# A hybrid attention layer in fp32: FF weight sums issued two per split in the attention stages, and the first gate's activation sums made in the GLA stage

## The chip, the cores and the metric

The kernel runs on one core of one Trainium2 chip, in one launch. The metric is the device time of that launch in microseconds, as the median of the runs. TensorE is called PE here, VectorE DVE, ScalarE ACT, GpSimd POOL and SyncE SP, as in the profile.

## What is computed

One layer of a streaming encoder, batch 1, 512 frames, width 1024, all in float32. Three branches read the same normalised input and are merged by gates; an FF block follows.

```python
u = rmsnorm(h, g_mix)
(gq, gk, gv, gg, ga, fq, fk, fv, ff, mq, gates) = split_cols(u @ w_in, PROJ_SIZES)
o_gla = gla_chunk_causal(gq, gk, gv, log_a)          # 4 heads, dk 64, dv 128
y_gla = (rmsnorm(o_gla, g_gla_head) * silu(gg)) @ w_gla_o
y_fox = forgetting_attention(fq, fk, fv, log_f) @ w_fox_o      # 8 heads of 64
y_mem = memory_attention(mq, mk, mv) @ w_mem_o       # 4 heads, 256 memory tokens
gt = sigmoid(gates)                                  # 3 gates of width 1024
merged = gt[0] * y_gla + gt[1] * y_fox + gt[2] * y_mem
h = h + merged @ w_out
u2 = rmsnorm(h, g_ffn)
h = h + square(relu(u2 @ w_ff1)) @ w_ff2
out = rmsnorm(h, g_final)
```

## The kernel before

**Precision.** Every fp32 product is made of three matmuls in `float32r` (`mm3`, L165 to L167): an operand x is split into hi = cast(x) and lo = x - hi, and hi*hi, hi*lo and lo*hi are added up in PSUM. A weight chunk is 128 x 1024 numbers, 512 KB. `load_w` (L148) loads it on SP's queue into `raw`, ACT casts `hi` (L155), DVE subtracts `lo` (L156). The three tags each have a ring of three tiles. The split of one chunk is followed by `next_sum` (L117), of which more below. The splits are counted from 1 (`chunk_n`).

**Stages.** The order of the program: the memory keys and values and the norm of x ("front"); FoX (`xp`); memory attention (`ap`); the GLA stage (`lp`); the gate stage (`op_`); FF (`yp`). In FoX, memory attention and the GLA stage, generators of projections (`gT`, `gN`, `outputs`) are woven with the steps of the attention (`weave`), in an order written out by hand, and ACT, DVE and SP follow program order as far as the scheduler leaves it. In the gate stage, `in_order` (L133) chains DVE, ACT and SP in program order. POOL's order is the scheduler's.

**The gate stage.** The three gates (fox, mem, gla, g = 0 to 2) are products of 512 x 1024 by 1024 x 1024, each made as seven products of half the size (Strassen in Winograd's form). `rounds` holds the order: (g, n) with n in (1, 2, 5, 3, 6, 7, 4), for g = 0, 1, 2, then ("Y", 1), (2, 4), ("Y", 0), ("O", 1), ("O", 0), where Y is the `w_gla_o` product and O the `w_out` product. A round of a gate has two weight chunks c, each with 24 matmuls for its tokens. The weights of rounds 1, 2 and 3 are blocks of `w_in`, the others are sums of blocks, made in two pairs of tiles `wb`: `load_sum` (L1060, SP) loads "11" or "12" into a tile, `plus` (L1063) adds another block by an accumulating DMA on POOL, and each round's split (`high` L1078 on ACT, `low` L1082 on DVE) reads the tile. In the first gate, `first_sum` (L1183) makes the first sum on DVE (`vec`, L1039) out of the two loaded tiles. The activations have sums too: S1 to S4 are splits (`left`, L1035 and L1036) of sums of the quarters of u, of which `sum_four` and `sum_three` make two. What of this is loaded and made in which round stands in the tables `loads`, `early` and `after`, filled by `at` and run round by round; in each round the evictions (`evac`), the tanh and the merges of the round before come in between.

**FF weight sums.** FF is Winograd too, and its weight sums are made in DRAM ahead of it: `sum_ops` (L107) lists for each of five blocks q eight DMAs on POOL, four copies and four accumulates, into the tensors T1 to T4. Blocks q = 1, 2, 3 take 1024 KB a DMA, q = 0 and 4 take 512 KB; 40 DMAs in all. `next_sum` issues one of them at each split from the eighth on, with a wait on that split's cast ("pace", L118 to L130). The list is cut in three: the first 32, then 4 from round (2, 6) on, the last 4 from round Y0 on, where two go with each split.

The sums are read in FF, where T is loaded like a weight (L1385).

## Time and profile before

| | us |
|---|---|
| median of 3 runs | 834.33 (832.12 to 834.57) |
| the profiled execution | 834.19 |
| its span | 832.4 |
| outside the span | 1.8 |

| stretch of the span | us, about |
|---|---|
| front | 0 to 45 |
| FoX | 45 to 158 |
| memory attention | 158 to 232 |
| GLA stage | 232 to 293 |
| first gate | 293 to 350 |
| second and third gate, Y and O | 350 to 490 |
| FF | 490 to 832 |

The page has, from the top: the busy time of each engine; the span in 40 slices of 20.8 us with one digit for tenths of busy time, the granted TensorE clock, and the DMA share; the DMA queues (q0 holds what POOL issues, q1 what SP and others issue by hardware); the chain of work that ended last; the groups of instructions by line and tile names. A row such as "PE mm L165 <- ACT ct L1133: 3.0, 1, 3.0" reads: PE waited at line 165 for ACT's line 1133, 3.0 us in total, once, at most 3.0. In the chain each row is a start, a duration and what ran.

### The profile page before, as it was taken

What the parts mean: (1) busy time and instruction counts of PE and PEld (TensorE: products, weight loads), DVE (VectorE), ACT (ScalarE), POOL (GpSimd) and SP (SyncE); (2) the same over time, 40 slices, a digit from 0 to 9 for tenths busy, and PEclk for the clock granted to TensorE, in tenths of its full rate; (3) what the DMA queues carried; (4) which work ended last, traced back from release to release, by engine and by line L of the source; (5) the groups of instructions that cost most, each with busy time, mean ns of one, the idle gap of its engine ahead of it and who ended that gap; (6) DMA issues with size and microseconds to landing.
All of it is one profiled execution on the core that took longest, in us unless ns stands there. A gap on an engine that the chain in (4) does not pass through costs nothing.

```text
span 832.4 us, 11709 instructions
## 1 busy us (share of the span) xinstructions
PE 805.4 (97%) x4375; PEld 685.6 (82%) x4375; DVE 609.3 (73%) x945; ACT 460.6 (55%) x733; POOL 101.2 (12%) x135
## 2 busy tenths in 40 slices
PE   9999999999999996988999999999999999999996
PEld 7788888888888874766888889998998899889985
DVE  6868887376455764746756656889799779888896
ACT  7757565434543433633553435786577366747764
POOL 0001010101011202123411000011001100110011
PEclk9999999999999997999999999999999999999998
DMA  9355565689586899885978642698867975896644
GB/s 358 130 171 177 178 178 159 186 238 278 138 230 190 263 247 228 210 177 163 216 177 284 187 149 76 214 283 184 264 195 160 219 238 173 192 233 230 172 79 128
DMA packets 40778, 165.44 MB, mean 199 GB/s; under 512 B 4881, under 2 KB 5585, under 8 KB 38353
## 3 DMA queue, kind: packets, MB, share of 16 engines
q0 software_dynamic: 10784, 61.87, 35.4%
q1 hardware_dynamic: 28576, 98.86, 33.8%
q10 hardware_dynamic: 1360, 3.96, 1.4%
q8 instruction: 34, 0.56, 0.3%
q14 instruction: 24, 0.19, 0.1%
HBM read 162.55 MB, written 35.68 MB: 238 GB/s over the span
## 4 chain that ended last, share of the span: by engine, by line
PE 83%; DMA 7%; DVE 4%; issue 3%; ACT 1%; POOL 1%; SPq 0%; POOLq 0%; DVEq 0%; ACTq 0%
PE mm L1317 15%; PE mm L165 14%; PE mm L167 14%; PE mm L166 14%; PE a L166 5%; PE a L167 5%; PE a L165 5%; DMA wb<-in_wst_dram 4%; PE mm L1646 3%; DMA raw<-in_wst_dram 1%; PE mm L1647 1%; DMA xt<-in_xT_dram 1%; DVE lo L1082 1%; PE mm L606 1%; PE a L399 1%
## 5 line engine op out<-in xcount | busy, mean ns | idle before, releaser
L1376 ACT CAST hi<-raw 128x1024 fp32r<-128x1024 f32 x52 | 54.5, 1048 | 36.9 <-PE mm L1317 16.2
L1377 DVE TENSOR_TENSOR lo<-raw,hi 128x1024 fp32r<-128x1024 f32 x52 | 63.6, 1224 | 14.4 <-ACT hi L1376 14.2
L156 DVE TENSOR_TENSOR wlo<-raw,whi 128x1024 fp32r<-128x1024 f32 x38 | 46.5, 1224 | 33.1 <-ACT whi L155 32.9
L1317 PE MATMUL mm<-u,hi 128*128 128x256 f32 x384 | 65.1, 283 | 0.0
L155 ACT CAST whi<-raw 128x1024 fp32r<-128x1024 f32 x38 | 39.9, 1050 | 41.3 <-PE mm L166 14.5
L165 PE MATMUL mm<-uhl,whi 128*128 128x512 f32 x144 | 57.8, 402 | 0.0
L1696 POOL DMA_DIRECT2D b<-in_wst_dram x30 | 25.6, 854 | 261.2 <-DVE lo L1377 130.3
L1317 PEld LDWEIGHTS mm<-u,hi 128*128 128x128 f32 x384 | 56.8, 191 | 0.3
L167 PE MATMUL mm<-uhl,wlo 128*128 128x512 f32 x144 | 56.3, 391 | 0.0
L166 PE MATMUL mm<-uhl,whi 128*128 128x512 f32 x144 | 56.2, 390 | 0.0
L165 PE MATMUL mm<-hi,ch 128*128 128x512 f32 (+1 forms) x132 | 50.9, 386 | 0.0
L166 PE MATMUL mm<-lo,ch 128*128 128x512 f32 (+1 forms) x132 | 50.9, 386 | 0.0
L167 PE MATMUL mm<-hi,cl 128*128 128x512 f32 (+1 forms) x132 | 50.9, 386 | 0.0
L1082 DVE TENSOR_TENSOR lo<-wb,hi 128x1024 fp32r<-128x1024 f32 x21 | 29.4, 1414 | 25.3 <-ACT hi L1078 25.2
L1317 PE MATMUL mm<-u2s,hi 128*128 128x256 f32 x288 | 47.6, 283 | 0.0
L1317 PE MATMUL mm<-u,lo 128*128 128x256 f32 x192 | 47.5, 283 | 0.0
L1376 ACT CAST hi<-b 128x1024 fp32r<-128x1024 f32 x26 | 27.3, 1049 | 29.5 <-PE mm L167 19.4
L1078 ACT CAST hi<-wb 128x1024 fp32r<-128x1024 f32 x28 | 28.6, 1046 | 25.8 <-DMA wb<-in_wst_dram 20.3
L1317 PEld LDWEIGHTS mm<-u2s,hi 128*128 128x128 f32 x288 | 41.8, 192 | 0.3
L1377 DVE TENSOR_TENSOR lo<-b,hi 128x1024 fp32r<-128x1024 f32 x26 | 31.7, 1224 | 10.9 <-ACT hi L1376 10.8
L166 PE MATMUL a<-lo,ch 128*128 128x512 f32 (+1 forms) x96 | 37.0, 385 | 0.0
L165 PE MATMUL a<-hi,ch 128*128 128x512 f32 (+1 forms) x96 | 37.0, 385 | 0.0
(501 smaller groups left out, 2335.9 us busy)
## 6 DMA issues: line engine op xcount, KB each, us to landing
raw<-in_wst_dram SPq DMA_DIRECT2D x110, 512.0 KB
raw<-T SPq DMA_DIRECT2D x32, 512.0 KB
b<-in_wst_dram POOLq DMA_DIRECT2D x32, 512.0 KB, 5.6
T<-in_wst_dram POOLq DMA_DIRECT2D x12, 1024.0 KB, 9.5
wb<-in_wst_dram POOLq DMA_DIRECT2D x22, 512.0 KB, 7.2
b<-in_wst_dram SPq DMA_DIRECT2D x16, 512.0 KB
T<-in_wst_dram POOLq DMA_DIRECT2D x12, 512.0 KB, 5.2
wb<-in_wst_dram SPq DMA_DIRECT2D x12, 512.0 KB
```

Of the source, the lines that this page charges most:

```text
L155: cast = nc.scalar.copy(hi, raw)
L156: low_now[0] = nc.vector.tensor_tensor(lo, raw, f(hi), op=ALU.subtract).ins
L165: nc.tensor.matmul(ps, lh, rh, start=start, stop=False, skip_group_check=on)
L166: nc.tensor.matmul(ps, lh, rl, start=False, stop=False, skip_group_check=on)
L167: nc.tensor.matmul(ps, ll, rh, start=False, stop=stop, skip_group_check=on)
L1078: next_sum(nc.scalar.copy(ws[r, c][0], source(r, c)).ins)
L1082: nc.vector.tensor_tensor(lo, source(r, c), f(hi), op=ALU.subtract)
L1317: nc.tensor.matmul(ps[:, a, :], x[:, a, k, :], y[:, s, k, :], start=start, stop=stop, skip_group_check=go is not None)
L1376: split_now[0] = nc.scalar.copy(hi, raw).ins
L1377: split_now[1] = nc.vector.tensor_tensor(lo, raw, f(hi), op=ALU.subtract).ins
L1646: nc.tensor.matmul(ps, wh[:, a, k, :], u[:, :, k, :], start=k == 0, stop=False, skip_group_check=True)
L1696: nc.gpsimd.dma_start(to[i], wst[index["B", q, i, x]], accum_op=ALU.add)
```

## The change

Three things:

1. `sum_ops` runs over the kind of sum in the outer loop and over the blocks q in the inner one. `next_sum` issues two DMAs at each split. The list is cut in two: 35 come in the splits from the eighth on, and the last five, the accumulates of "21" into T4, come from Y0 on. The cut at round (2, 6) is gone. With two at a split, the 35 are issued at splits 8 to 25.
2. The splits S1 and S4 of the first gate (with `sum_four`) are made in the GLA stage by `u_lefts`, in four tiles (`omt`) that the memory outputs leave free. So that these are free, the outputs of the memory branch come ahead of `gla_g(2)`. S2 keeps its tile, and the tile pairs of every fourth split are `own_tile(0)` now.
3. The first gate doesn't load its "11" blocks again: `first_sum` adds the "12" tile to the `raw` tile of the split that was made ready in the GLA stage. The weights of round (0, 2) are loaded straight into the `wb` tiles that are free for that. In every gate the "22" accumulate now stands after round (g, 5), and the load ahead of it at (g, 4) of the gate before.

POOL's order, in the GLA stage and the first gate: `T_3_89` to `T_3_92` are the sums T1 to T4 of block q = 3, `stat` is the GLA norm, and `wb` are the gate's sum tiles. Before:

```order
L126 DMA T_3_89<-in_wst_dram 128x2048
L971 TENSOR_TENSOR stat_2435<-stat_2435,mhalf 128x4 x2
L126 DMA T_3_91<-in_wst_dram 128x2048
L128 DMA T_3_90<-T_3_89 16x16384
L126 DMA T_3_90<-in_wst_dram 128x2048
L1063 DMA wb_2987<-in_wst_dram 128x1024
L128 DMA T_3_92<-T_3_90 16x16384
L1063 DMA wb_2988<-in_wst_dram 128x1024
L1063 DMA wb_2985<-in_wst_dram 128x1024
L1063 DMA wb_2986<-in_wst_dram 128x1024
L126 DMA T_3_92<-in_wst_dram 128x2048
L1063 DMA wb_2985<-in_wst_dram 128x1024
```

After (the number behind `T_` is the block q; here L126 is a copy and L1074 the gate's accumulate, since the lines have moved):

```order
L126 DMA T_4_96<-T_4_94 16x8192
L126 DMA T_1_84<-T_1_82 16x16384
L126 DMA T_2_88<-T_2_86 16x16384
L126 DMA T_3_92<-T_3_90 16x16384
L939 MEMSET at_2557 128x512
L939 MEMSET at_2558 128x512
L897 MEMSET ex_2453 128x8
L897 MEMSET ex_2610 128x8
L939 MEMSET at_2728 128x512
L939 MEMSET at_2729 128x512
L969 TENSOR_TENSOR stat_2447<-stat_2447,mhalf 128x4 x4
L1074 DMA wb_2995<-in_wst_dram 128x1024
```

The sums have left the rows between the GLA norm and the gate's accumulates; the last copies stand ahead of the first memset of the GLA stage (`at`).

DVE's order at the end of the GLA stage, before (`on` is the normed head before PE's transpose, `og` the gated head, `wlo` a weight split):

```order
L974 TENSOR_SCALAR on_2711<-a_2681,stat_2435 128x128 x4
L934 TENSOR_SCALAR mid_2744<-mid_2744,stat_2435 128x128
L156 TENSOR_TENSOR wlo_2788<-raw_2785,whi_2787 128x1024
L156 TENSOR_TENSOR wlo_2905<-raw_2902,whi_2904 128x1024
L982 TENSOR_TENSOR og_2807<-a_2802,sg_116 128x512
L219 TENSOR_TENSOR og_2428<-og_2807,og_2428 128x512
L982 TENSOR_TENSOR og_2816<-a_2811,sg_117 128x512
L219 TENSOR_TENSOR og_2429<-og_2816,og_2429 128x512
L969 TENSOR_REDUCE stat_2435<-sq_2850 128x4
L970 TENSOR_SCALAR stat_2435<-stat_2435 128x4
L969 TENSOR_REDUCE stat_2435<-sq_2860 128x4
L974 TENSOR_SCALAR on_2855<-a_2834,stat_2435 128x128 x4
```

And after (`s` are the low halves of S1 and S4, `x` the sum that becomes S4):

```order
L980 TENSOR_TENSOR og_2814<-a_2809,sg_117 128x512
L217 TENSOR_TENSOR s_2918<-x_2285,s_2917 128x1024
L154 TENSOR_TENSOR wlo_2910<-raw_2907,whi_2909 128x1024
L997 TENSOR_TENSOR x_2285<-x_2381,uhl 128x1024
L217 TENSOR_TENSOR og_2441<-og_2814,og_2441 128x512
L997 TENSOR_TENSOR x_2285<-x_2285,uhl 128x1024
L967 TENSOR_REDUCE stat_2447<-sq_2848 128x4
L154 TENSOR_TENSOR wlo_2930<-raw_2927,whi_2929 128x1024
L968 TENSOR_SCALAR stat_2447<-stat_2447 128x4
L217 TENSOR_TENSOR s_2924<-x_2285,s_2923 128x1024
L967 TENSOR_REDUCE stat_2447<-sq_2858 128x4
L972 TENSOR_SCALAR on_2853<-a_2832,stat_2447 128x128 x4
```

Two subtractions and two additions of 128 x 1024 now stand there, ahead of the `on` of the last two heads.

DVE's order at the start of the first gate, before (`f0l` is the low half of S1, `f2l` that of S4, `lo` and `f3l` weight splits, `ct` the evictions):

```order
L1036 TENSOR_TENSOR f0l_2980<-x_2272,f0h_2979 128x1024
L1082 TENSOR_TENSOR lo_3016<-raw_2993,hi_3015 128x1024
L1082 TENSOR_TENSOR f3l_3021<-raw_2995,hi_3020 128x1024
L1039 TENSOR_TENSOR wb_2985<-wb_2985,wb_2987 128x1024
L1039 TENSOR_TENSOR wb_2986<-wb_2986,wb_2988 128x1024
L1082 TENSOR_TENSOR lo_3061<-wb_2985,hi_3060 128x1024
L1082 TENSOR_TENSOR lo_3067<-wb_2986,hi_3066 128x1024
L1039 TENSOR_TENSOR x_2272<-x_2369,uhl 128x1024
L1039 TENSOR_TENSOR x_2272<-x_2272,uhl 128x1024
L1039 TENSOR_TENSOR ct_3041<-ct_3041,a_3046 128x512
L1039 TENSOR_TENSOR ct_3041<-ct_3041,a_3047 128x512
L1036 TENSOR_TENSOR f2l_2984<-x_2272,f2h_2983 128x1024
```

And after:

```order
L1091 TENSOR_TENSOR lo_3016<-wb_2993,hi_3015 128x1024
L1091 TENSOR_TENSOR f0l_3020<-wb_2994,f0h_3019 128x1024
L1050 TENSOR_TENSOR wb_2993<-raw_2927,wb_2995 128x1024
L1050 TENSOR_TENSOR wb_2994<-raw_2967,wb_2996 128x1024
L1091 TENSOR_TENSOR lo_3059<-wb_2993,hi_3058 128x1024
L1091 TENSOR_TENSOR lo_3064<-wb_2994,hi_3063 128x1024
L1050 TENSOR_TENSOR ct_3037<-ct_3037,a_3044 128x512
L1050 TENSOR_TENSOR ct_3037<-ct_3037,a_3045 128x512
L1165 SCALAR_TENSOR_TENSOR acc_1815<-ct_3037,acc_1815 128x512
```

The activations' halves and sums have left these rows; the second row's `f0l` is now the low half of a weight chunk, and the first sum reads a `raw` tile.

The diff:

```diff
@@ -105,22 +105,20 @@
     tsum = {(n, q): dram.tile([2 if 0 < q < 4 else 1, P, 1024], F32, name=f"T{n}_{q}") for q in range(5) for n in (1, 2, 3, 4)}
 
     def sum_ops():
-        for q in range(5):
-            for n, src, add in ((1, "11", 0), (3, "12", 0), (1, "12", 1), (3, "22", 1), (2, 1, 0), (2, "22", 1), (4, 2, 0),
-                                (4, "21", 1)):
+        for n, src, add in ((1, "11", 0), (3, "12", 0), (1, "12", 1), (3, "22", 1), (2, 1, 0), (2, "22", 1), (4, 2, 0), (4, "21", 1)):
+            for q in (0, 4, 1, 2, 3):
                 i = index["F", q % 4, 0 if q else 1, src] if isinstance(src, str) else None
                 yield tsum[n, q], tsum[src, q] if i is None else wst[i:i + (2 if 0 < q < 4 else 1)], add
 
-    sums = [islice(sum_ops(), *x) for x in ((32,), (32, 36), (36, None))]
+    sums = [islice(sum_ops(), *x) for x in ((35,), (35, None))]
     late_on, merged, chunk_n, cast_now, low_now, hold = [], [None], [0], [None], [None], [None]
 
     def next_sum(after):
 
         chunk_n[0] += 1
-        n = chunk_n[0]
-        if n <= 7:
+        if chunk_n[0] <= 7:
             return
-        for to, src, add_ in islice(sums[len(late_on)], 1 + (len(late_on) == 1)):
+        for to, src, add_ in islice(sums[len(late_on)], 2):
             with tc.issue_after(merged[0]) if late_on else ExitStack():
                 if add_:
                     d = nc.gpsimd.dma_start(to, src, accum_op=ALU.add, max_dma_last_dim=8192)
@@ -762,8 +760,8 @@
     xsp = mst.enter_context(pool("sums", side="right"))
     omst = ExitStack()
     omp = omst.enter_context(pool("omem", side="right"))
-    omh = [omp.tile([P, S], F32R, name=f"omh{j}") for j in range(4)]
-    oml = [omp.tile([P, S], F32R, name=f"oml{j}") for j in range(4)]
+    omt = [omp.tile([P, 2, S], F32R, tag=f"om{j}", name=f"om{j}") for j in range(4)]
+    omh, oml = ([x[:, i] for x in omt] for i in range(2))
 
     def half_of(t, c):
         return t[:, 512 * c:512 * c + 512]
@@ -982,17 +980,29 @@
             nc.vector.tensor_tensor(og, pt, sg[h], op=ALU.mult)
             split(ogh[h], ogl[h], og)
 
-        ready = []
+        ready, lefts = [], {}
 
         def gate_ready(n):
-            ready.append(get_w(gate_key("gate_fox", 1, n)))
+            raw = load_w(gate_key("gate_fox", 1, n))
+            ready.append((raw, split_w(raw)))
+
+        def u_left(n, x):
+            to = [omp.tile([P, 1024], F32R, tag=f"om{j}", name=nm("s")) for j in ((0, 1) if n == 1 else (2, 3))]
+            lefts[n] = [t.rearrange("p (k t) -> p k t", k=4) for t in to]
+            split(*lefts[n], x)
+
+        def u_lefts():
+            u_left(1, xsum[1])
+            for y, z in ((xsum[2], A12[0]), (xsum[1], A12[1])):
+                nc.vector.tensor_tensor(xsum[1], y, z, op=ALU.add)
+            u_left(4, xsum[1])
 
         steps = (
             (decays, (0,), 13), (key_turn, (0,), 5), (gla_scores, (0,), 2), (decays, (1,), 9), (key_turn, (1,), 4),
             (gla_values, (0,), 0), (gla_scores, (1,), 8), (gla_turn, (0,), 0), (gla_turn, (1,), 4), (gla_values, (1,), 10),
-            (gate_ready, (0,), 0), (gla_turn, (2,), 6), (gate_ready, (1,), 0), (gla_turn, (3,), 0))
-        weave([partial(fn, *a) for fn, a, _ in steps], 64, gla_k(1), gla_q(1), gla_g(2, lp, "og"),
-              outputs("w_mem_o", omh, oml, ymem), gla_g(3, lp, "og"), shares=[n for *_, n in steps])
+            (u_lefts, (), 0), (gate_ready, (0,), 0), (gla_turn, (2,), 6), (gate_ready, (1,), 0), (gla_turn, (3,), 0))
+        weave([partial(fn, *a) for fn, a, _ in steps], 64, gla_k(1), gla_q(1),
+              outputs("w_mem_o", omh, oml, ymem), gla_g(2, lp, "og"), gla_g(3, lp, "og"), shares=[n for *_, n in steps])
     gst.close()
 
 
@@ -1025,7 +1035,8 @@
 
 
         quad = lambda t: t.rearrange("p (k t) -> p k t", k=4)
-        S1, S2, S4 = ([quad(own_tile(i, g)) for g in "hl"] for i in range(3))
+        S1, S4 = (lefts[n] for n in (1, 4))
+        S2 = [quad(own_tile(1, g)) for g in "hl"]
         S3 = [t[:, 0:4, 256:512] for t in (uhi, ulo)]
         GATE = {1: [t[:, 0:4, 0:256] for t in (uhi, ulo)], 2: [t[:, 4:8, 0:256] for t in (uhi, ulo)],
                 4: [t[:, 4:8, 256:512] for t in (uhi, ulo)], 5: S1, 6: S2, 3: S4, 7: S3}
@@ -1069,8 +1080,6 @@
             split_n[0] += 1
             if split_n[0] % 4:
                 return [wp.tile([P, 1024], F32R, tag=x, name=nm(x)) for x in ("hi", "lo")]
-            if rounds.index(now[0]) < at_round["Y", 0]:
-                return hp.tile([P, D], F32R, tag="gf", name=nm("hi")), own_tile(3, "l")
             return [own_tile(0, x) for x in "hl"]
 
         def high(r, c):
@@ -1171,19 +1180,13 @@
             nc.scalar.mul(h, pt, 0.5)
             nc.vector.scalar_tensor_tensor(l, pt, 0.5, f(h), op0=ALU.mult, op1=ALU.subtract)
 
-        def sum_four():
-            vec(xsum[1], xsum[2], A12[0])
-            vec(xsum[1], xsum[1], A12[1])
-
         def sum_three():
             x = xsum[2]
             nc.vector.scalar_tensor_tensor(x, x, -1.0, A22[0], op0=ALU.mult, op1=ALU.subtract)
             vec(x, x, A22[1], ALU.subtract)
 
         def first_sum(n):
-            x = sum_tile(0, n, 0)
-            vec(x, x, sum_tile(0, n, 1))
-            plus(0, n, 1, "22")
+            vec(sum_tile(0, n, 0), ready[n][0], sum_tile(0, n, 1))
 
         def res_evac(c):
             def go(t, ps):
@@ -1208,34 +1211,35 @@
 
         for g in range(3):
             for c in range(2):
-                at(loads, (g, 1), get, (g, 2), c, shift=-3)
+                if g:
+                    at(loads, (g, 1), get, (g, 2), c, shift=-3)
             for c in range(2):
-                at(loads, (g, 1), get, (g, 3), c, shift=c)
+                at(loads, (g, 1), get, (g, 3), c, shift=c if g else 1)
+                at(after, (g, 5), plus, g, c, 1, "22")
                 if g < 2:
                     at(loads, (g, 7), load_sum, g + 1, c, 0)
-                    at(loads, (g + 1, 1), load_sum, g + 1, c, 1)
-                    at(loads, (g + 1, 1), plus, g + 1, c, 1, "22")
+                    at(loads, (g, 4), load_sum, g + 1, c, 1)
         for r, back in ((("Y", 1), -4), (("Y", 0), -2), (("O", 1), -2), (("O", 0), -2)):
             for c in range(2):
                 at(loads, r, get, r, c, shift=back)
-        for r, fn, *args in (((0, 1), left, S1, xsum[1]), ((0, 1), first_sum, 0), ((0, 1), first_sum, 1), ((0, 2), sum_four),
-                             ((0, 5), left, S4, xsum[1]), ((0, 3), left, S2, xsum[2]), ((0, 3), sum_three),
+        for r, fn, *args in (((0, 1), first_sum, 0), ((0, 1), first_sum, 1), ((0, 5), left, S2, xsum[2]), ((0, 5), sum_three),
                              ((0, 6), left, S3, xsum[2])):
-            at(early if fn is left else after, r, fn, *args)
-        at(after, (2, 6), late_on.append, 1)
+            at(early if r[1] == 6 else after, r, fn, *args)
 
         def go(when, i):
             for fn, args in when.get(i, []):
                 fn(*args)
 
-        ws.update({((0, 1), n): w for n, w in enumerate(ready)})
+        ws.update({((0, 1), n): w for n, (_, w) in enumerate(ready)})
         split_n[0] = 2
         mh = ml = None
         hN, now = [], [rounds[0]]
         with in_order():
             for n in range(2):
-                for other in range(2):
-                    load_sum(0, n, other)
+                load_sum(0, n, 1)
+            for n in range(2):
+                raws[(0, 2), n] = sum_tile(0, n, 0)
+                nc.sync.dma_start(raws[(0, 2), n], wst[index[gate_key("gate_fox", 2, n)]])
             for i, r in enumerate(rounds):
                 now[0] = r
                 if r == (2, 7):
```

## The prediction

> **What bounds the kernel now.** I read the page's list of engines first, then its two rows on the TensorE clock and the DMA load, then the span cut into stretches, the waits of PE and the chain of waits inside the stretch that loses most.
>
> ```profile
> PE 805.4 (97%) x4375; PEld 685.6 (82%) x4375; DVE 609.3 (73%) x945; ACT 460.6 (55%) x733; POOL 101.2 (12%) x135
> PEclk9999999999999997999999999999999999999998
> DMA  9355565689586899885978642698867975896644
> ```
>
> PE is busy for 97% of the span, so what can be won at the end is only what PE loses, and it loses little: 27 us of idle time and some time at a lower clock. Both rows of digits show one place. The 16th slice (312 to 333 us, a slice being 20.8 us) is the only inner one in which the granted clock drops to 7 tenths, and the DMA engines are at 8 and 9 tenths around it. That is the first gate. The same place in stretches of 10 us:
>
> ```profile
> 290.00:300.00 10.00, 9.49 (x44) 7.53 (x42) 5.90 (x8) 3.12 (x4) 0.00 (x0) 1.00 0.97 281
> 300.00:310.00 10.00, 8.88 (x36) 6.79 (x37) 8.23 (x9) 4.12 (x5) 1.71 (x2) 1.00 0.91 227
> 310.00:320.00 10.00, 6.30 (x20) 4.54 (x19) 7.03 (x8) 5.80 (x7) 3.20 (x4) 0.81 0.92 206
> 320.00:330.00 10.00, 7.24 (x24) 5.08 (x22) 1.49 (x2) 2.10 (x2) 1.71 (x2) 0.84 1.07 240
> 330.00:340.00 10.00, 9.44 (x29) 7.14 (x29) 8.02 (x8) 4.81 (x6) 0.86 (x1) 0.66 0.95 211
> ```
>
> The columns are PE, PEld, DVE, ACT and POOL busy with their counts, then the granted clock, the DMA share and GB/s. PE is idle for 0.51 + 1.12 + 3.70 + 2.76 + 0.56 = 8.65 us. The clock columns lose another 10 x (0.19 + 0.16 + 0.34) = 6.9 us. Together the first gate loses 15.6 us, and the DMA share is over 0.9 in every row. The waits and the chain say why.
>
> ```profile
> PE mm L165 <- ACT ct L1133: 3.0, 1, 3.0
> PE mm L166 <- DVE lo L1082: 2.0, 3, 0.8
> PE mm L165 <- ACT hi L1078: 2.0, 1, 2.0
> ```
>
> ```profile
> 288.44 12.22 DMA raw<-in_wst_dram
> ...
> 303.05 2.51 DMA T<-in_wst_dram
> 305.55 7.77 issue
> ...
> 313.34 0.52 POOL T L128
> 313.86 1.12 POOL wb L1063 x2
> 314.98 13.60 DMA wb<-in_wst_dram
> ...
> 328.65 1.06 ACT hi L1078
> 329.74 1.23 DVE lo L1082
> 330.96 1.15 DVE x L1180
> 332.13 1.24 DVE x L1039
> 333.39 1.05 ACT uhl L1035
> 342.75 3.25 DMA wb<-in_wst_dram
> ```
>
> PE waits for split weights (`hi`, `lo`) and for an eviction that stands behind them on ACT. Behind the splits stand a plain load that took 12.22 us and an accumulate (`wb`) that took 13.60 us. The last row is a plain load of 512 KB with little beside it: 3.25 us. Ahead of the accumulate on POOL stands a weight sum `T`, for which POOL sat until 313.34. So the first gate waits for DMA work of the FF sums, twice: in POOL's queue and on the DMA engines.
>
> **What the change removes there.** No `T` is issued between the GLA stage and Y0 any more, so neither the 7.77 us in POOL's queue nor the sums' bytes stand before the gate's accumulates. The gate also has two loads fewer, its "22" accumulates come a round or two later, and the four splits and sums for S1 and S4 (in the chain: the `x` adds of 1.24 us, a cast of 1.05 us) leave its DVE and ACT. All of 15.6 us can go. What is late next is the gate's own accumulates:
>
> ```profile
> wb<-in_wst_dram POOLq DMA_DIRECT2D x22, 512.0 KB, 7.2
> ```
>
> 7.2 us is their median landing, while a round is 48 matmuls here, about 10.4 us (44 of them took 9.49 us in the first of the five rows). A pair that is issued together and lands one after the other could be up to 3 us late, or never. I take 1.5 us, range 0 to 4. Term: -15.6 + 1.5 = **-14.1 us**. Gates 2 and 3 keep POOL's order, so their stalls stay:
>
> ```profile
> PE mm L165 <- DVE ct L1039: 4.8, 2, 3.5
> ```
>
> These two waits (in the stretch from 340 to 400 us) hang on the tanh and merge chain, which the change doesn't touch: 0.
>
> **Where the sums go.** They must be paid on the DMA engines elsewhere. What do they cost?
>
> ```profile
> q0 software_dynamic: 10784, 61.87, 35.4%
> q1 hardware_dynamic: 28576, 98.86, 33.8%
> T<-in_wst_dram POOLq DMA_DIRECT2D x12, 1024.0 KB, 9.5
> T<-in_wst_dram POOLq DMA_DIRECT2D x12, 512.0 KB, 5.2
> T<-T POOLq DMA_DIRECT2D x4, 512.0 KB, 4.4
> ```
>
> Plain loads are on q1: 0.338 x 832.4 / 98.86 = 2.85 us of all 16 engines for a million bytes. Everything that POOL issues is on q0: 0.354 x 832.4 = 294.7 us for 61.87. Of these, the 16 MB of `T` copies are 16.8 million bytes; at the price of a plain load they take 47.9 us, and the rest, all accumulates, (294.7 - 47.9) / 45.1 = 5.5 us for a million.
>
> ```profile
> 80.00:120.00 40.00, 40.00 (x233) 33.12 (x232) 33.77 (x103) 24.12 (x58) 3.38 (x5) 1.00 0.63 189
> 120.00:158.00 38.00, 38.00 (x210) 32.07 (x209) 25.28 (x61) 19.33 (x42) 3.10 (x5) 1.00 0.57 175
> 158.00:204.00 46.00, 46.00 (x229) 38.94 (x228) 28.05 (x44) 20.39 (x41) 4.95 (x8) 1.00 0.85 229
> ```
>
> From 80 to 204 us (FoX and memory attention, splits 8 to 25) PE is busy without a gap and the DMA engines work 0.63 x 40 + 0.57 x 38 + 0.85 x 46 = 86 us of 124. In that stretch before issues 18 sums: 8.4 million bytes of copies and 6.3 of adds, 23.9 + 34.7 = 58.6 us. So the rest of the work (weight loads, the decay rows) is 27.4 us. After issues 35 there: 16.8 of copies and 12.6 of adds, 47.9 + 69.3 = 117 us. Together that is **144.6 us of DMA work in 124 us**: 20.6 us too much. The copies of T1 and T3 come first and fit; from the fifth paced split on (119 us) the ten adds of T1 and T3 alone are 46 us against 31 us in which they are issued. From there the DMA engines are never idle, until about 225 us.
>
> POOL itself has the time: 17 issues more of under 0.9 us each, on an engine that is 12% busy, and nothing but sums stands in its queue there. Nobody waits for a sum before FF. What waits is the weight loads.
>
> ```profile
> L148 SPq DMA_DIRECT2D raw<-in_wst_dram x15: 327/328/332, 123.7 to 221.6; - x15
> L148 SPq DMA_DIRECT2D raw<-in_wst_dram x9: 327/328/332, 151.8 to 204.9; - x9
> L155 ACT CAST whi<-raw x9: 1047/1054/1056, 169.3 to 230.6; 128x1024 fp32r<-128x1024 f32 x9
> PE mm L165 <- DVE at L949: 0.9, 1, 0.9
> ```
>
> The first three rows are the loads from 119 to 231 us, the last nine of them up to 205 us, and the casts of those nine. A load comes every 7.0 us ((221.6 - 123.7) / 14), and its cast starts 17.5 us (151.8 to 169.3) to 25.7 us (204.9 to 230.6) after its issue. The last row is the only wait of PE on others between 78 and 290 us. So before, a load of 3.25 us has 14 us to spare. In after it has sums beside it all the time. Its landing lies between that and the 12.22 us of the chain's load, issued among a sum copy and an add: the middle is 7.7 us, a little over the 7.0 us at which loads come. At 7.7 us nothing is late: 17.5 us cover it, and a backlog of 0.7 us at each of 15 loads is 10 us. At 12.22 us the loads fall 5.2 us further behind at each split, and the 14 us are gone after three. They can't all be that slow, since the work exceeds the time by 20.6 us only. So the price on PE lies between 0 and 20.6 - 14 + a few us for what stands behind a late cast, 12 us. ACT runs in program order: behind a cast that waits for its `raw` stand the casts and exponentials of memory attention (`ph`, `Pm`, `omh`), and PE waits for these. That makes the upper half more than a theory; against it speaks that casts run a ring ahead of PE. I take **+5 us**, nearer the lower end.
>
> The Trainium skill, page "DMA: Bandwidth & Descriptors", section "Queues, rings and completion order", says that each DMA engine takes turns between the queues that have work and drains a whole packet of one before it goes to the next, which speaks against long packets beside short ones: the trace agrees in that one load took 12.22 us beside sums and another 3.25 us. With the means of the queue rows (294.7 x 16 / 10784 = 0.44 us for a packet of q0, 0.16 us and 3.46 KB for one of q1), equal turns would let the 152 packets of a load through 16 engines in 9.5 turns, 5.7 us, by which this term would be 0 and the sum 822.3 us; that is an estimate by the page's rule, and case B below gives the same without it.
>
> **The other edits.**
>
> ```profile
> 255.00:290.00 35.00, 34.08 (x221) 28.63 (x220) 23.55 (x49) 14.41 (x22) 9.32 (x13) 1.00 0.73 225
> ```
>
> In the GLA stage two casts and four DVE operations for S1 and S4 now stand in DVE's order ahead of `on` of the last two heads: 2 x 1.23 + 2 x 1.24 = 4.9 us on DVE. PE's last GLA transposes wait for these `on`. PE has weights ready there and DVE is idle for a third of this row, so I take 1.2 us, between 0 and the 4.9 us if nothing hides it. `w_mem_o` goes ahead of `gla_g(2)`: the same work in another order, 0. The five adds that stay:
>
> ```profile
> 430.00:460.00 30.00, 30.00 (x140) 24.84 (x139) 19.32 (x24) 12.30 (x15) 3.18 (x5) 1.00 0.77 260
> 460.00:490.00 30.00, 30.00 (x144) 24.76 (x143) 18.84 (x26) 13.74 (x22) 2.07 (x3) 1.00 0.60 177
> ```
>
> Before issues its last eight sums there, half-size ones, and PE is never idle; after has 4.2 million bytes of adds (23 us) instead of about 17.5 us of work, with 60 x 0.32 = 19 us to spare. 0 to 3 us, I take 1, for they come two at a time beside the loads for `w_out`.
>
> **The sum.** The profiled execution took 834.19 us, 832.4 of it the span; it agrees with the median of 834.33 us. 834.2 - 14.1 + 5 + 1.2 + 1 = **827.3 us**.
>
> **The rivals.**
> A, the sum above: the gate's stall goes, part of it comes back at the late casts in memory attention. 822 to 832 us.
> B, no cast is ever late: the term of 5 is 0, 834.2 - 14.1 + 1.2 + 1 = 822.3 us; with the smaller terms at 0 as well, 818.6. For it: 14 us to spare, PE without a wait. Against it: 20.6 us more DMA work than time.
> C, slower: the loads come in only as the sums drain. Then the overload lands on PE in full, about 18 to 21 us from some 170 us on, ACT held by a cast whose `raw` is late, and the clock falls in the longer gaps as it does in the first gate. 834.2 - 14.1 + 2.2 + 18 = 840.3 us. It decides once PE loses more than 11.9 us there. For it: the load of 12.22 us. Against it: copies, which hold the engines longest, are only 16.8 of 29.4 million bytes and half of them come early, when there is room.
> D, the gate's stall is its own: with the sums away its accumulates still land in 13 us as they queue on each other, so that two thirds of the 15.6 us stay; 834.2 - 5 + 2.2 + 2 = 833.4 us. For it: 13.60 us for an accumulate and a stretch at 1.07 of DMA share in which only one sum runs. Against it: their median of 7.2 us.
>
> On the clock: at 316 us and again at 330 us PE was slowed after gaps of 3 us, rows 0.81, 0.84 and 0.66. The Trainium skill, page "TensorE: Matmul & The Clock Gate", section "What's actually happening", says that after an idle window of about 3.4 us the array runs at half rate until it has been busy for such a window; the rows agree, since 6.9 us were lost by the clock beside 8.65 us of idle time. By this rule a wait of 5 us in one piece in memory attention would cost up to 1.7 us more, split in short ones nothing.
>
> **How the numbers follow.** A 0.50, B 0.22, C 0.14, D 0.14. The range reaches from the low end of B to just past the point from which C decides: 818.5 to 836 us. It leaves out most of C and little of B, under 2 in 10. A measurement of this kernel can tell about 0.3% from no change, 2.5 us: under 831.8 counts as faster, above 836.8 as slower. A and B are faster but for the upper end of A (0.03); of D a third is faster. Faster 0.73, same 0.14, slower 0.13.
>
> **What would show it.** In the changed profile: no `T` among the gate's accumulates, PE nearly full and the clock at 1.00 from 290 to 340 us, `wb` landing in 5 to 7 us. DMA share of 0.95 or more from 125 to 220 us. The casts of the later splits idle before a `raw` load, and PE waiting for ACT or `whi` between 170 and 235 us for some 5 us. I am wrong if PE has no wait there (B), waits over 12 us or shows a clock under 0.9 (C), or if the first gate still waits for `wb` (D).

## The result and the profile after

The changed kernel takes 828.88 us (median of 12 runs, 823.02 to 831.51), the kernel before 834.56 us (12 runs, 832.12 to 838.20). The ratio is 0.9924, with a 95% interval of 0.9904 to 0.9945, so the change is worth 6.3 us (4.6 to 8.0). The forecast was 827.3 us, 7.0 us faster. The profiled execution took 827.70 us, 825.9 of it the span.

The page's head after the change:

```profile
PE 800.9 (97%) x4375; PEld 681.3 (82%) x4375; DVE 607.5 (74%) x945; ACT 459.6 (56%) x733; POOL 102.9 (12%) x135
PEclk9999999999999999999999999999999999999998
DMA  9354879999922229866937932798857865896643
```

The dip of the clock in the 16th slice is gone. On the DMA row the load has moved: the 7th to 11th slices (124 to 227 us) are at 9 tenths now, the four behind them (227 to 310 us, the GLA stage and the start of the first gate) at 2. The first gate, in the same stretches as before:

```profile
290.00:300.00 10.00, 10.00 (x48) 8.13 (x47) 7.35 (x16) 3.07 (x6) 1.91 (x1) 1.00 0.03 12
300.00:310.00 10.00, 9.90 (x44) 7.84 (x43) 8.62 (x10) 5.78 (x8) 3.56 (x4) 1.00 0.47 111
310.00:320.00 10.00, 8.94 (x38) 6.68 (x36) 7.38 (x8) 4.76 (x6) 0.00 (x0) 1.00 1.05 242
320.00:330.00 10.00, 8.23 (x34) 6.07 (x34) 6.86 (x7) 5.52 (x7) 1.72 (x2) 1.00 0.79 156
330.00:340.00 10.00, 8.65 (x39) 6.85 (x38) 8.30 (x11) 5.86 (x7) 0.86 (x1) 1.00 0.71 233
```

PE is idle for 4.3 us in these 50 us instead of 8.65, and the clock stays at 1.00. The kernel is further on as well: the last row is now the end of the first gate. The same stage by what PE does in it: matmuls in the five rows are 203 instead of 153.

The longest of PE's waits in them (290 to 340 us):

```profile
PE mm L164 <- DVE lo L1091: 1.5, 2, 0.8
PE mm L163 <- DVE ct L1050: 1.3, 1, 1.3
PE mm L163 <- ACT hi L1087: 1.0, 2, 0.7
```

To compare stages whose places differ, I count PE's lost time from the starts of the matmuls in the trace: each distance from start to start beyond what the same pair takes without a wait (0.23 us for 512 columns), the half-speed matmuls included. The sums of this count differ between kernels as their spans do (before to after 7.0 us in the count, 6.5 us in the span; before to the fastest order below 16.0 in both).

| us lost by PE | FoX | memory attention | GLA | first gate | second gate to round (1, 3) | second gate from round (1, 6) | third gate, Y, O, FF | all, front included |
|---|---|---|---|---|---|---|---|---|
| before | 0.0 | 0.0 | 2.7 | 17.7 | 5.4 | 5.8 | 0.0 | 32.6 |
| after | 1.8 | 0.0 | 2.7 | 5.8 | 6.5 | 5.2 | 2.5 | 25.6 |

PE's waits in FoX, memory attention and the GLA stage (80 to 290 us) after the change:

```profile
PE a L695 <- DVE PTl L217: 1.5, 2, 1.3
PE mm L163 <- DVE at L947: 0.9, 1, 0.9
```

There is one new wait, in FoX, and none in memory attention, where the forecast had 5 us. Among the waits of ACT (80 to 232 us) and of DVE (80 to 158 us), these are the ones for a transfer:

```profile
ACT whi L153 <- DMA raw<-in_wst_dram: 2.6, 1, 2.6
```

```profile
DVE nFb L640 <- DMA nFb<-dF: 4.2, 2, 2.9
```

One cast waited for its load, 2.6 us, once. In FoX, DVE waited 4.2 us for the decay rows (2.6 before), and `PTl`, for which PE waited, stands behind that in DVE's order. The DMA engines were as full as the sum said:

```profile
80.00:158.00 78.00, 76.48 (x432) 63.30 (x431) 56.83 (x161) 41.74 (x96) 13.30 (x20) 1.00 0.90 273
158.00:232.00 74.00, 74.00 (x368) 62.56 (x368) 43.40 (x76) 35.13 (x75) 10.27 (x17) 1.00 0.96 285
```

```profile
T<-in_wst_dram POOLq DMA_DIRECT2D x12, 1024.0 KB, 17.4
T<-T POOLq DMA_DIRECT2D x4, 512.0 KB, 20.1
wb<-in_wst_dram POOLq DMA_DIRECT2D x22, 512.0 KB, 6.7
```

The load is at 0.90 and 0.96, and the sums took the delay: 17.4 us from issue to landing where it was 9.5, and 20.1 where it was 4.4. What is left of the first gate's stall stands in its chain of waits (300 to 325 us):

```profile
304.70 1.84 POOL wb L1074 x2
...
306.77 14.74 DMA wb<-in_wst_dram x2
...
321.59 1.06 ACT hi L1087
```

Four accumulates, two by two, and PE waits for the second two, of which the last lands 14.74 us behind the issue of the first. They are for round (0, 6). The two ahead of them in that queue are the "22" on the other tile pair, which is not read until the weights of round (0, 7) are split, one round later.

### The profile page after: what moved, and what is told of

Same layout as the page of the kernel before. It is cut to its first block, busy times and chain, and to the rows that moved or that the text cites. A ratio compares the mean times of both kernels' runs of the same rounds, so it can differ in the third digit from the quotient of the medians.

```text
span 825.9 us, 11694 instructions
## 1 busy us (share of the span) xinstructions
PE 800.9 (97%) x4375; PEld 681.3 (82%) x4375; DVE 607.5 (74%) x945; ACT 459.6 (56%) x733; POOL 102.9 (12%) x135
## 4 chain that ended last, share of the span: by engine, by line
PE 45%; DMA 8%; DVE 5%; issue 4%; ACT 2%; POOL 0%; POOLq 0%; SPq 0%; DVEq 0%; ACTq 0%
PE mm L1321 11%; PE mm L164 7%; PE mm L165 7%; PE mm L163 7%; DMA wb<-in_wst_dram 4%; PE a L164 3%; PE a L165 3%; PE a L163 3%; PE mm L1650 3%; DMA b<-in_wst_dram 2%; DMA raw<-in_wst_dram 2%; PE mm L1651 1%; DVE lo L1091 1%; DVE lo L1438 1%; DVE f0l L1091 0%
## 5 line engine op out<-in xcount | busy, mean ns | idle before, releaser
L1700 POOL DMA_DIRECT2D b<-in_wst_dram x30 | 25.6, 855 | 265.3 <-DVE lo L1381 131.1
L165 PE MATMUL a<-hi,cl 128*128 128x512 f32 (+1 forms) x96 | 37.0, 385 | 0.0
## 6 DMA issues: line engine op xcount, KB each, us to landing
T<-in_wst_dram POOLq DMA_DIRECT2D x12, 1024.0 KB, 17.4
```

What stands on the lines that cost most here:

```text
L165: nc.tensor.matmul(ps, ll, rh, start=False, stop=stop, skip_group_check=on)
L1700: nc.gpsimd.dma_start(to[i], wst[index["B", q, i, x]], accum_op=ALU.add)
```

## The experiments

Each time stands beside runs of the kernel before on the same chip, and the comparisons go by the ratio. Every kernel computes the whole layer.

**The sums alone.** The kernel before, with `sum_ops`, `next_sum` and the cut of the list as in the changed kernel and nothing else:

```diff
-    sums = [islice(sum_ops(), *x) for x in ((32,), (32, 36), (36, None))]
+    sums = [islice(sum_ops(), *x) for x in ((35,), (35, None))]
...
-        for to, src, add_ in islice(sums[len(late_on)], 1 + (len(late_on) == 1)):
+        for to, src, add_ in islice(sums[len(late_on)], 2):
...
-        at(after, (2, 6), late_on.append, 1)
```

> The kernel before with the first part of the change alone: the sums run by kind, two per split, 35 ahead of the gates and five from Y0 on; the gate stage and the GLA stage are as before. My theory: the first gate's stall came from the sums in POOL's queue and on the DMA engines, so this alone has most of the gain: PE's lost time in the first gate falls from 17.7 us to about 7 (1 to 3 us more than after keeps, since the S1 and S4 work and two loads are still there), the 1.8 us in FoX appear: 829 us beside 834.5, ratio 0.992 to 0.996. The rival, that the edits of the gate stage bring the gain: this one is at 834 to 836, ratio 1.000 to 1.003.

Measured: 829.3 us beside 836.12, ratio 0.991 (0.9891 to 0.993). The loss in the first gate is 7.8 us, and its cost is 1.6 us in FoX and 1.4 in memory attention. The waits of PE from 80 to 290 us that the kernel before doesn't have:

```profile
PE a L695 <- DVE PTl L217: 1.4, 1, 1.4
PE a L163 <- DVE pl L217: 1.2, 1, 1.2
```

By the ratio, the sums alone have all of the gain that the whole change has; the spans of the profiled executions say 4.9 us of 6.5.

**The gate edits alone.** The changed kernel with the old `sum_ops`, `next_sum` and cuts, the reverse of the diff above.

> The changed kernel with the sums of before: one per split, by blocks, four of them from round (2, 6) on; S1, S4, the ready weights and the two loads fewer stay. My theory: the sums still stand ahead of the gate's accumulates, and the first gate loses 10 to 14 us of PE: 831 to 833 us, ratio 0.995 to 0.998. The rival, that the edits of the gate stage bring the gain: 827 to 829, ratio 0.991 to 0.994, and the first gate loses 6 us.

Measured: 829.87 us, ratio 0.9921 (0.9902 to 0.994): the number of the rival. But its place is my theory's, for the first gate still loses 12.7 us, of which the wait for a cast behind an accumulate is the largest; the two longest of PE's waits from 290 to 345 us:

```profile
PE mm L165 <- ACT hi L1089: 3.9, 1, 3.9
PE mm L165 <- ACT ct L1144: 2.2, 1, 2.2
```

So both halves gain, 5.0 us here with nothing lost in FoX, and they don't add up: 7.5 and 6.6 us by the ratios alone, 6.3 together. Neither theory had said that. Something that they share had to bound the whole.

**Small pieces.** The changed kernel, with the copies of the sums cut as the accumulates are:

```diff
-                    d = nc.gpsimd.dma_start(to, src)
+                    d = nc.gpsimd.dma_start(to, src, max_dma_last_dim=8192)
```

> The changed kernel with the copies of the sums cut into pieces of 8 KB as the accumulates are; before each piece was 32 or 64 KB. Theory: the 1.8 us that PE lost in FoX came from the decay rows that waited behind large pieces on each DMA engine; with small pieces the rows' loads get their turn, the wait of DVE for nFb falls from 4.2 to 2.6 us or less and the loss in FoX goes: 1 to 2 us faster than the changed kernel, 826.5 to 828. Rival: it is the amount of bytes or the moved order of the nFb additions, and nothing changes in FoX: 828.5 to 829.5; or small pieces cost so much more that the DMA engines are late in memory attention: 830 or more.

Measured: 830.3 us, ratio 0.9928 (0.9908 to 0.9948), the same as the changed kernel's 0.9924. FoX loses 1.5 us. DVE's wait for the decay rows, in the rows for `nFb`:

```profile
  DMA nFb<-dF: 4.6, 2
```

4.6 us beside 4.2: the size of the pieces isn't the cause. My theory of the large pieces fell.

**The next round's accumulates first.** The changed kernel with the "22" on the other pair (read for round (g, 7)) held behind the gate's own "22" (read for round (g, 6)):

```diff
+        own_plus = {}
...
         def plus(g, n, other, b):
-            nc.gpsimd.dma_start(sum_tile(g, n, other), wst[index[gate_key(GATES[g], b, n)]], accum_op=ALU.add)
+            with tc.issue_after(own_plus[g]) if other else ExitStack():
+                d = nc.gpsimd.dma_start(sum_tile(g, n, other), wst[index[gate_key(GATES[g], b, n)]], accum_op=ALU.add)
+            if b == "22" and not other:
+                own_plus[g] = d.ins
```

> The changed kernel with another order of the gates' accumulates on POOL: in each gate the two accumulates of 22 on the other pair, needed three rounds later, come behind the two that the next round needs, where POOL had them ahead. Theory: what is left of the stall in the first gate (5.8 us) and at the start of the second (6.5 us) is these four landing one after the other (up to 13.6 us); with the two that are needed first ahead, they land in some 7 us, and 5 to 9 us go: 820 to 824 us. Rival: the accumulates of the first pair wait for the split that reads their tile, and landing is set by loads on the other queue: at most 2 us, 827 to 829.

Measured: 818.24 us (818.08 to 819.52) beside 836.12, ratio 0.9784 (0.9763 to 0.9806), lower than all that I had expected. The first gate loses 3.1 us and the second, up to round (1, 3), 0.8. POOL's queue in the first gate, before this edit (the changed kernel) and with it:

```profile
304.70 1.84 POOL L1074 DMA_DIRECT2D wb<-in_wst_dram  x2 [12.15 <-issue]
306.77 0.85 POOL L1074 DMA_DIRECT2D wb<-in_wst_dram  x1 [0.23 <-DVE lo L1091]
307.91 0.86 POOL L1074 DMA_DIRECT2D wb<-in_wst_dram  x1 [0.29 <-DVE lo L1091]
321.23 0.86 POOL L1074 DMA_DIRECT2D wb<-in_wst_dram  x1 [12.45 <-DVE lo L1091]
```

```profile
307.13 0.94 POOL L1076 DMA_DIRECT2D wb<-in_wst_dram  x1 [14.24 <-DVE lo L1095]
308.27 2.63 POOL L1076 DMA_DIRECT2D wb<-in_wst_dram  x3 [0.19 <-issue]
318.94 0.86 POOL L1076 DMA_DIRECT2D wb<-in_wst_dram  x1 [8.04 <-DVE lo L1095]
```

The four accumulates stand together in both. With the edit the next step of the chain is issued at 318.94 instead of 321.23 us, though the first of the four went out 2.4 us later: two of four places in the queue were worth 4.7 us. And the stretches of the first gate:

```profile
310.00:320.00 10.00, 9.60 (x43) 7.63 (x42) 9.65 (x10) 7.10 (x9) 1.76 (x3) 1.00 1.02 215
320.00:330.00 10.00, 9.84 (x44) 7.83 (x43) 6.56 (x8) 6.15 (x7) 0.86 (x1) 1.00 0.99 247
```

PE is nearly full at a DMA load of 1.02 and 0.99. The DMA engines weren't short; the order in one queue was wrong.

**The order alone, and the order with the gate edits.** The same edit on the kernel before, and on the gate edits with the old sums. In the kernel before the "22" on the other pair also moves behind round (g, 5), as the change has it, so this kernel has a little of the gate edits.

> The kernel before with nothing but the other order of the gates' accumulates on POOL (those of the next round ahead of those needed three rounds later); its sums and its gate work stay. Theory Q, that the gates' losses are a matter of what lands first on one DMA queue, and that the change took other things off that queue: the second gate's loss of 5.4 us goes, and of the first gate's 17.7 us some 5 go, the sums still stand ahead: 823 to 827 us beside 834.5 to 836, ratio 0.988 to 0.992. Rival, that the sums and the gate's own work on DVE and ACT make the first gate's stall: only the second gate gains, ratio 0.993 to 0.996.

Measured: 830.75 us beside 835.87, ratio 0.9943 (0.9922 to 0.9963). The first gate loses 19.4 us. That is the rival's number and the rival's place: the second gate gains (2.7 us up to round (1, 3) instead of 5.4), the first doesn't. Only part of the number has a place, though: the ratio says 4.8 us, and the two profiled executions differ by 1.6 us in their spans (830.8 and 832.4).

> The gate edits of the change and the other order of the accumulates, with the sums issued as before, four of them still ahead of or among the first gate's accumulates. It tells what moving the sums is worth once the accumulates are in order. Theory Q: the first gate still loses 2 to 5 us more than with the sums moved (3.1 us), but FoX loses nothing (1.4 us): 818 to 823 us, ratio 0.978 to 0.985. Rival, that the sums are what makes the stall: the first gate loses 8 us or more, ratio 0.986 or higher.

Measured: 828.76 us, ratio 0.9918 (0.9902 to 0.9933). The first gate loses 14.3 us: the rival's case. The longest wait of PE from 290 to 345 us, and POOL's queue:

```profile
PE mm L165 <- DVE ct L1052: 7.0, 1, 7.0
```

```profile
300.72 0.87 POOL L126 DMA_DIRECT2D T<-in_wst_dram  x1 [8.95 <-ACT hi L1093]
309.02 0.52 POOL L128 DMA_DIRECT2D T<-T  x1 [7.44 <-DMA T<-in_wst_dram]
309.53 3.60 POOL L1078 DMA_DIRECT2D wb<-in_wst_dram  x4
315.47 0.83 POOL L126 DMA_DIRECT2D T<-in_wst_dram  x1 [2.34 <-DMA T<-T]
320.24 0.87 POOL L1078 DMA_DIRECT2D wb<-in_wst_dram  x1 [3.94 <-DVE lo L1097]
324.07 0.86 POOL L1078 DMA_DIRECT2D wb<-in_wst_dram  x1 [2.95 <-DVE lo L1097]
```

POOL sits 7.44 us for a sum that must land before its next copy, four accumulates go out late, and a sum of 1 MB stands at 315.47 between them and the two that come last. The last one's landing, in the chain of waits:

```profile
324.07 14.80 DMA wb<-in_wst_dram
```

With the gate edits alone the longest stall stood in front of round (0, 6); here it stands in front of round (0, 4), as one wait of 7.0 us. So beside the gate edits the order is worth nothing that can be measured while the sums stand in the queue (6.8 us won, 6.6 without it).

**The sums and the order without the gate edits.**

> The kernel before with the sums moved as in the change and the other order of the accumulates, but without the edits of the gate stage (S1, S4, the ready weights, two loads fewer). Theory: with the DMA queue free and in order, the gate's own loads and its DVE and ACT work set what is left; the edits are then worth the 2 us by which the first gate lost more without them: 820 to 823 us, ratio 0.980 to 0.985. Rival, that they are worth nothing once the accumulates land in time: 818 to 819, ratio 0.977 to 0.980.

Measured: 822.61 us beside 835.47, ratio 0.9845 (0.9832 to 0.9859): the theory's bracket, at its upper end. The first gate loses 7.8 us, 4.7 more than with the gate edits, not 2. With it, each of the three parts is there with and without the others, but for the later "22", which comes with the gate edits and with the order alike (us won by the ratio, on 834.5; in brackets by the spans of the profiled executions, one for each kernel):

| | sums as before | sums moved |
|---|---|---|
| nothing else | 0 | 7.5 (4.9) |
| gate edits | 6.6 (5.1) | 6.3 (6.5), the change |
| order | 4.8 (1.6) | 12.9 (12.3) |
| gate edits and order | 6.8 (5.9) | 18.0 (16.0) |

The moved sums are worth 11.2 us where the rest is in order (10.1 by the spans), and nothing measurable where the gate edits stand without the order (6.3 beside 6.6, each to about 1.7). What in the gate edits gains wasn't tried apart: the halves of S1 and S4 made earlier, the two loads fewer, or the later "22".

**Three sums per split, later.** The changed kernel with the order, and:

```diff
-        if chunk_n[0] <= 7:
+        if chunk_n[0] <= 13:
             return
-        for to, src, add_ in islice(sums[len(late_on)], 2):
+        for to, src, add_ in islice(sums[len(late_on)], 2 if late_on else 3):
```

> The changed kernel with the other order of the accumulates, and its 35 sums started at split 14 (126 us) instead of split 8, three per split: 117 us of DMA work for sums in the 78 us to split 25, beside loads, some 60 us more than the time. If each load gets its turn beside the sums (case B's reason), PE loses under 2 us in memory attention all the same, FoX loses nothing and the sums land by 265 us or so, ahead of the gates: 816.5 to 819 us, ratio 0.976 to 0.980. If the loads come in as the sums drain (rival C), PE loses 10 to 30 us from 160 us on: 828 to 850 us.

Measured: 828.29 us beside 835.87, ratio 0.9911 (0.9895 to 0.9928). In FoX and memory attention PE loses nothing, and the GLA stage loses 14.3 us. The time is at the edge of what I had for rival C, but not in its place. The stretch of memory attention, ACT's wait for loads from 120 to 240 us, PE's longest wait from 80 to 290 us and POOL's queue around the end of the sums:

```profile
158.00:232.00 74.00, 74.00 (x369) 62.67 (x368) 42.28 (x73) 34.52 (x74) 13.76 (x19) 1.00 1.01 265
```

```profile
ACT whi L153 <- DMA raw<-in_wst_dram: 8.0, 3, 4.5
```

```profile
PE a L912 <- DVE kn L900: 10.4, 1, 10.4
```

```profile
194.30 0.49 POOL L126 DMA_DIRECT2D T<-T  x1 [3.06 <-DMA T<-in_wst_dram]
214.53 0.82 POOL L124 DMA_DIRECT2D T<-in_wst_dram  x1 [19.74 <-DMA T<-T]
...
250.90 0.49 POOL L126 DMA_DIRECT2D T<-T  x1 [5.62 <-DMA T<-in_wst_dram]
251.38 1.01 POOL L939 MEMSET at<- 128x512 f32 x2
252.31 0.13 POOL L897 MEMSET ex<- 128x8 f32 x1
```

With the DMA engines full for 74 us, casts waited three times, 8.0 us in all, and PE still never. The loads get their turn, as case B had it. What broke is something that I had not listed: POOL executes in order, an accumulate into T waits for the copy before it to land (19.74 us at 214.53), and a memset of the GLA stage, 0.13 us of work, stood behind them until 252.31. PE waited 10.4 us for the product behind it. The changed kernel is clear of this; the last row of its POOL queue ahead of the memsets:

```profile
215.11 0.49 POOL L126 DMA_DIRECT2D T<-T  x1 [5.78 <-DMA T<-in_wst_dram]
```

Its last sum before the gates is out at 215 us.

**Fewer sums in FoX.** The changed kernel with the order, and one sum at splits 8 to 12, three at 13 to 16, two from there.

> The changed kernel with the other order of the accumulates, and one sum at each of splits 8 to 12, three at 13 to 16, two from there: the same 35 by split 25. Theory: PE's loss in FoX (1.4 us) is made by the sums that are on the DMA engines when the decay rows are loaded, and goes; nothing is lost in memory attention, and POOL has issued its last sum ahead of the GLA stage's memsets: 816 to 818 us, ratio 0.975 to 0.979, 1 to 1.5 us better than the other order alone. Rival: POOL is held by its earlier sums until after 240 us, PE waits for the memset in the GLA stage as it did with three per split from split 14: 819 to 825.

Measured: 818.95 us beside 835.47, ratio 0.9805 (0.9788 to 0.9821). FoX loses 1.4 us as it did. Neither the theory's gain nor the rival's wait in the GLA stage came (2.7 us are lost there, as in the others); the interval overlaps that of the order alone. With no sum before split 14 (the run above) FoX lost 0.0, and in the kernel before, with one sum per split in another order, also 0.0. So the loss goes with the sums that are in flight there, but neither the pieces' size nor two at a time explains it, and it isn't the same in every execution: PE's wait for `PTl` is 0.5 us with the old sums, the gate edits and the order, and 0.5 us as well with two sums per split and the order. The first eight sums of the kernel before are half-size ones (block 0); what their size does wasn't tried. The cause stays open.

**The merge on DVE.** The changed kernel with the order, and:

```diff
-                merged[0] = nc.gpsimd.tensor_tensor(a, a, x, op=ALU.add).ins
+                merged[0] = nc.vector.tensor_tensor(a, a, x, op=ALU.add).ins
```

> The changed kernel with the other order of the accumulates, and the additions of the second gate's merge on DVE instead of POOL. Theory: the last stall of over 3 us (PE for DVE, at the end of the second gate, 5.1 us with the clock) is long since DVE's subtractions take 2.3 us instead of 1.2 beside POOL's additions; on DVE these cost 2 x 0.6 us in its order, and the stall shrinks by 1 to 2.5 us: 816 to 817.5 us. Rival: the additions stand ahead of the split that PE waits for and it is later by what they take: 818 to 820.

Measured: 816.38 us (813.67 to 820.22) beside 835.47, ratio 0.9772 (0.9745 to 0.9799). The low halves at the end of the second gate, with the additions on POOL and then on DVE:

```profile
L1095 DVE TENSOR_TENSOR lo<-wb,hi x4: 1224/1772/2320, 360.5 to 377.9; 128x1024 fp32r<-128x1024 f32 x4
```

```profile
L1095 DVE TENSOR_TENSOR lo<-wb,hi x3: 1216/1224/1225, 358.8 to 369.6; 128x1024 fp32r<-128x1024 f32 x3
```

The subtractions are back at 1.22 us and the longest wait of PE is 2.8 us instead of 3.5. But the interval holds the ratio of the order alone (0.9784), and the loss counted from round (1, 6) to the end of the second gate isn't smaller (5.9 beside 5.1 us, the clock's share included). That the kernel is faster by it is not shown.

## Why the prediction was right

The number held: 828.2 us by the ratio on 834.5, where 827.3 was forecast, and the interval of the ratio excludes no change. Its parts held less well.

- *The first gate, -14.1 us.* Measured -11.9 (17.7 to 5.8 us), mechanism and place as said, the size a little off. What should be late next was named rightly, the gate's own accumulates that land one after the other. Of the 5.8 us about 3.6 are theirs, at round (0, 6); some 1.5 are a wait for `ct` at round (0, 4) that the kernel before has too. The 1.5 us for the accumulates was mis-sized, and the step that has it wrong is the length of a round. The prediction took 48 matmuls and 10.4 us; a round is 24 matmuls for both chunks together (two token tiles, two chunks, two halves of a chunk, three matmuls), about 5.5 us: in the changed kernel's trace round (0, 5) starts at 307.31 us and round (0, 3) at 313.28. The kernel's description has the same slip, with 24 for each chunk. A landing of 7.2 us is longer than such a round, and the two that PE waits for took 14.74 us. It is the mechanism of rival D, at about a third of the price that D gave it (3.6 us, D had 10).
- *That no `T` before the gates is what does it.* Right only in part. The sums alone gain 7.5 us, but the gate edits without them gain 6.6. I had worked out the stall as if one cause were behind it; the eight kernels of the table show three things that count: the sums in POOL's queue, the gate edits as a whole, and the order of the gate's accumulates in that queue. By the ratio, only with the order put right do the two parts of the change add up to more than either alone.
- *Memory attention, +5 us.* This step failed: measured 0.0. The DMA load was as worked out (0.96 where the sum said full), and one cast waited 2.6 us. The failed step is the price, drawn between 0 and 12 us from a load that took 12.22 us beside sums, as if loads wait their turn behind them. The landing times of the sums show where the backlog went: to the sums themselves, 9.5 to 17.4 us. The Trainium skill, page "DMA: Bandwidth & Descriptors", section "Queues, rings and completion order", has engines take turns between queues; this term would have been 0 by it, and the traces agree, at 0.96 and at 1.01 of DMA share alike.
- *FoX.* Not in the sum: 1.8 us. The decay rows were counted among "the rest of the work" but not as something that DVE, in order, waits for.
- *The GLA stage, +1.2 us.* Measured 0.0 (2.7 us in both). DVE had the time for the four operations: it is busy for 36.3 of the 58 us from 232 to 290.
- *Y and O, +1 us.* In Y, O and FF together 2.5 us are lost that weren't before, 1.0 of them in O at the place named; every kernel with the moved sums loses about 1 us or more there, and none with the old ones. The other 1.5 us are two waits in FF near 560 us, for low halves. Ahead of the first of them the chain has two accumulates of FF's own, 12.20 us from the issue of the first to the landing of the second. The kernels with the sums in the old places lose up to 0.8 us there too, and no run tells why they are late.
- *Gates 2 and 3, 0.* Measured +1.1 in the second gate up to round (1, 3) and -0.6 from round (1, 6); no wait of PE in the third.
- *The clock.* The prediction has a wait of 5 us in one piece halve the clock and short ones cost nothing. Short ones did, in both kernels: in the row below, of the changed kernel, PE's waits are of 0.7 to 1.1 us, four of them close together at round (1, 5), and the granted clock is 0.86 there and 0.97 in the ten microseconds behind (0.87 and 0.96 in the kernel before, ten microseconds later). The price of 5 us in memory attention doesn't hang on it.

```profile
350.00:360.00 10.00, 6.62 (x20) 4.31 (x19) 4.10 (x5) 3.63 (x4) 1.73 (x2) 0.86 0.69 154
```

So 6.2 us of cost that didn't come (memory attention 5, the GLA stage 1.2) were made good by 6.6 us that did or weren't won: the first gate 2.2, FoX 1.8, FF 1.5, the second gate 1.1. The total is right partly by luck, and a reader should take the mechanism from the runs.

## What to carry to other kernels

Where a stage waits for transfers of one queue, look first at the order in that queue: put what is needed first ahead of what is needed later. Here this one dependency made 18.0 us out of the change's 6.3, with the DMA engines as busy as before. Parts of a change that gain the same alone as together may share a bound that none of them removes, and trying each with and without the others is the way to find it. Work that is moved to where the DMA engines are "free" costs what stands in order behind it on every engine: a wait on a landing held an unrelated memset on POOL for 14 us here (252.31 us, 238.42 in the changed kernel), and the additions to the decay rows held DVE's other work in FoX.

## What the runs showed of the hardware

- Weight loads on their own queue were in time beside a queue that kept the DMA engines at 1.01 for 74 us: PE lost nothing, casts 8.0 us. The transfers of the full queue paid: the 1 MB sums took 22.2 us to land there (median; 17.4 in the changed kernel, 9.5 before).
- Copies between DRAM tensors in pieces of 8 KB and of 32 or 64 KB made no difference that can be measured (ratios of 0.9928 and 0.9924).
- A DVE subtraction of 128 x 1024 took up to 2.32 us beside POOL's additions and 1.22 us without them.
- The granted clock fell (0.86 over 350 to 360 us) behind four waits of PE of at most 1.1 us each.
